# A decoder step on one core: the window's new scores join the other new scores, window rows are requested by GpSimd in front of the pages, and the stored tokens are loaded in two portions

## The chip, the cores and the metric

The kernel runs on one core of a Trainium2 chip. A core has a matrix engine (TensorE, PE in the profile), a vector engine (VectorE, DVE), a scalar engine (ScalarE, ACT), a general engine (GpSimd, POOL) and a queue engine that only issues transfers (SyncE, SP). Each engine works through its own row of instructions in order; semaphores tie them together. Transfers (DMA) can be requested from SyncE, ScalarE or GpSimd. The metric is the device time of one execution in microseconds; less is better.

## What is computed

The reference is one step of a hybrid decoder layer: a prompt of 512 tokens, and 8 other sequences that each get 8 new tokens on top of 2048 stored ones. Two attention branches run side by side, Fox (with forget gates) and NSA (compressed blocks, selected blocks, and a sliding window of 512), then gates merge them, and an MLP follows. What matters here is the part on the 8 sequences:

```python
PAST_LEN = 2048; PAGE_SIZE = 128; DEC_BATCH = 8; DEC_SEQ = 8; WINDOW = 512

def gather_pages(pool, page_table):
    g = pool[page_table]
    return g.reshape((g.shape[0], g.shape[1] * g.shape[2]) + g.shape[3:])

def fox_attend(q, cq, q_pos, k, v, ck, k_pos):
    s = jnp.einsum('btgrd,bsgd->bgrts', q, k).astype(jnp.float32) * HEAD_DIM ** -0.5
    ...
    p = masked_softmax(s + bias, k_pos[None, :] <= q_pos[:, None])
    return jnp.einsum('bgrts,bsgd->btgrd', p.astype(v.dtype), v)

def nsa_attend(q, q_pos, gates, kc, vc, c_end, ks_blk, vs_blk, kw, vw, w_pos):
    ...
    s = jnp.einsum('btgrd,bwgd->bgrtw', q, kw).astype(jnp.float32) * scale - m * dw.astype(jnp.float32)
    p_w = masked_softmax(s, (dw >= 0) & (dw < WINDOW) & (w_pos >= 0)[None, :])
    o_w = jnp.einsum('bgrtw,bwgd->btgrd', p_w.astype(vw.dtype), vw)
    return gates[..., 0:1] * o_c + gates[..., 1:2] * o_s + gates[..., 2:3] * o_w
```

## The kernel before, in words

The stage of the change is `sample_attention`. It handles the 8 sequences one after the other, b = 0 to 7; the sliding window is handled once for each pair, n = b // 2. For one sequence all stored keys and values of two kinds are brought in: Fox rows `fr` and the rows of the selected blocks `sr`, 2.1 MB each. They stand in three row buffers that rotate (b % 3), and are transposed in place by VectorE (`key_turn`) ahead of the scores.

The order on PE for one sequence is: `sequence_scores` (`ss`, 64 matmuls of 32 x 512 on the rows and 4 on `CT`), `new_scores` (`sn`, the new tokens against each other), on even sequences `window_new` (the window's new scores, into the right half of the same bank), then `values` of the sequence before (`so`, with rows and the transposed weights `spT`), on odd sequences the window's values (`so<-wr`) and the sums (`accS`), on even ones `window_keys` (`wk`, transposes of window rows `wr`). Last come the transposes of the softmax weights, `turn_weights` (`spn`, `sp`), which ScalarE copies out of the bank to `TN` and `spT`, and on even sequences the window's scores (`sw`).

`sample_load(b)` requests the rows of a sequence: four 512-KB loads of `fr` and sixteen 128-KB loads of `sr`, half on SyncE's queue and half on GpSimd's, two and eight each. `sample_load(b + 2)` stands behind `values(b - 1)`, whose matmuls are the last to read the buffer. `window_load` requests the window's rows of one sequence (512 KB); for the first pair GpSimd does it ahead of the loop, for the others ScalarE, at the end of an odd iteration. `key_prep` is two GpSimd instructions that prepare the forget counts of one sequence, and stands at the end of an iteration. `key_counts` and `key_turn` are VectorE's work on the next sequence, tied to be issued after the statistics of the current one.

The order of the instructions on an engine is set by a scheduler, which goes by the order of the code, priorities and the `issue_after` ties. A request is tied to the one before it on the same engine (`self.issued`), as `key_prep` is for GpSimd.

At the last sequence the mixer follows. Its input, the stored tokens, stands in DRAM (`hfd`) and is loaded into `hL` in eight parts of 288 KB, alternately by SyncE and GpSimd. ScalarE copies each part to `hH` with reduced digits, VectorE keeps the rest in `hL`. `mix_first` then multiplies the first gate group (`mg00`) in pairs of parts, in between the values of the last sequence; further gate groups (`mg01` and so on) follow in `mix_part`.

## Time and profile before

| what | us |
|---|---|
| median of 3 runs | 1208.71 |
| lowest and highest | 1204.95, 1223.38 |
| the profiled execution | 1212.07 |
| its span, first to last instruction | 1210.4 |
| the eight sequences | about 437 to 569 |

In the stage the windows of the profile, cut about at the scores of the sequences, show these shares of their length:

| window, us | length | PE busy | granted clock | DMA share |
|---|---|---|---|---|
| 437 to 453 | 16 | 14.27 | 0.95 | 1.00 |
| 453 to 470 | 17 | 15.05 | 0.85 | 0.58 |
| 470 to 485 | 15 | 12.13 | 1.00 | 0.99 |
| 485 to 502 | 17 | 15.06 | 1.00 | 0.84 |
| 502 to 515 | 13 | 10.98 | 0.87 | 1.03 |
| 515 to 531 | 16 | 15.07 | 1.00 | 0.98 |
| 531 to 551 | 20 | 15.31 | 0.57 | 0.59 |
| 551 to 569 | 18 | 16.74 | 1.00 | 0.63 |

How to read the views. A timeline row gives the start and duration, the engine, the code's line, the operation, what is written and read, shapes and a count; at its end in brackets stand the idle time of the engine ahead of it and what ended that. "issue" there means that nothing shown in the profile was waited for. PEld is PE's loading of weights. SPq and ACTq are the queues' own instructions, whose transfers land later. A row of waits gives the total in us, the number and the longest. A row of a tile gives count and min/median/max of the duration in ns. The clock is the share of full speed granted to PE. All 16 transfer engines together are a DMA share of 1.00.

### The profile page before, as it was taken

The numbers are of one execution on the slowest core, as the hardware profiler recorded it, in microseconds if no ns is written. First come the engines' busy times: TensorE is split into PE (matmuls) and PEld (weight loads), VectorE is DVE, ScalarE is ACT, GpSimd is POOL, SyncE is SP. The second block draws the span as 40 slices with busy tenths as digits, with TensorE's granted clock in tenths as the row PEclk, the third lists the DMA queues.
The fourth block names the chain that finished last, engine by engine and source line by source line (L and its number), as shares of the span: only waits on it lengthen the run. The fifth ranks groups of instructions, "written<-read, shape, count | busy, mean of one in ns | idle before, by whom it ended". The sixth has DMA issues, their size and how long they took to land. (4 is left out here: it accounts for less than half of the span.)

```text
span 1210.4 us, 24491 instructions
## 1 busy us (share of the span) xinstructions
PE 1134.3 (94%) x9305; PEld 972.1 (80%) x9305; DVE 686.4 (57%) x1743; ACT 508.9 (42%) x1062; POOL 194.5 (16%) x284
## 2 busy tenths in 40 slices
PE   3869999999999988888999999999999999999998
PEld 3867789988666545546999999988988989899896
DVE  6777666675788867656643437652343433333545
ACT  3446553444777644436422324464321313123230
POOL 6530000001211343330000000010201102011110
PEclk9989999999999899989999999999999999999999
DMA  9996485764876597994733333142322314223102
GB/s 222 281 262 179 144 256 187 231 208 129 276 237 202 180 279 264 325 323 133 184 81 94 79 96 106 42 118 85 106 71 70 105 35 137 66 78 97 43 18 79
DMA packets 164488, 184.68 MB, mean 153 GB/s; under 512 B 17386, under 2 KB 143795, under 8 KB 162195
## 3 DMA queue, kind: packets, MB, share of 16 engines
q1 hardware_dynamic: 141954, 137.63, 38.8%
q0 software_dynamic: 10832, 32.12, 8.2%
q10 hardware_dynamic: 11584, 13.37, 3.7%
q8 instruction: 73, 1.20, 0.4%
q14 instruction: 45, 0.36, 0.1%
HBM read 175.17 MB, written 28.81 MB: 169 GB/s over the span
## 5 line engine op out<-in xcount | busy, mean ns | idle before, releaser
L2049 POOL TENSOR_TENSOR u<-u 128x576 f32<-128x576 f32 x32 | 54.0, 1688 | 417.5 <-ACT u L112 327.9
L100 DVE TENSOR_TENSOR acc<-acc,dn 128x512 f32<-128x512 f32 x60 | 39.8, 686 | 78.0 <-PE dn L77 78.0
L77 PE MATMUL mg<-hH,wml 128*128 128x288 f32 x256 | 75.1, 295 | 0.0
L77 PE MATMUL mg<-hH,wmh 128*128 128x288 f32 x256 | 74.9, 295 | 0.0
L77 PE MATMUL mg<-hL,wmh 128*128 128x288 f32 x256 | 72.8, 294 | 0.0
L77 PE MATMUL hid<-xh,w1hlk 128*128 128x256 f32 (+1 forms) x192 | 47.6, 341 | 20.5 <-ACT xh L112 20.5
L783 DVE TENSOR_TENSOR u<-u,u 128x512 fp32r<-128x512 f32 x64 | 28.4, 484 | 63.0 <-ACT u L112 63.0
L77 PE MATMUL z<-winh,h2r 128*128 128x264 f32 (+1 forms) x288 | 57.8, 290 | 2.3 <-ACT adw L112 2.3
L112 ACT ACTIVATE xh<-cpg 128x512 fp32r<-128x512 f32 x64 | 37.4, 623 | 46.1 <-PE hid L77 29.6
L77 PE MATMUL z<-winh,h 128*128 128x264 f32 (+1 forms) x288 | 56.7, 287 | 0.0
L131 DVE TENSOR_TENSOR xl<-cpg,xh 128x512 fp32r<-128x512 f32 x64 | 42.5, 685 | 19.9 <-ACT xh L112 19.6
L131 DVE TENSOR_TENSOR wml<-wmr,wmh 128x1024 fp32r<-128x1024 f32 x16 | 19.6, 1224 | 59.0 <-ACT wmh L112 59.0
L77 PEld LDWEIGHTS hid<-xh,w1hlk 128*128 128x128 f32 x192 | 33.6, 203 | 23.7 <-ACT xh L112 20.5
L77 PE MATMUL hid<-xh,w1hlv 128*128 128x256 f32 (+1 forms) x192 | 47.0, 338 | 5.3 <-ACT csx L112 5.3
L77 PEld LDWEIGHTS z<-winh,h2r 128*128 128x128 f32 x288 | 45.8, 190 | 3.7 <-ACT adw L112 2.5
L77 PEld LDWEIGHTS mg<-hH,wmh 128*128 128x128 f32 x256 | 48.1, 188 | 0.2
L77 PEld LDWEIGHTS mg<-hH,wml 128*128 128x128 f32 x256 | 48.1, 188 | 0.0
L112 ACT ACTIVATE u<-up 128x256 f32<-128x256 f32 (+1 forms) x96 | 27.7, 324 | 46.9 <-PE up L77 46.8
L77 PEld LDWEIGHTS mg<-hL,wmh 128*128 128x128 f32 x256 | 47.3, 188 | 0.0
L77 PEld LDWEIGHTS z<-winh,h 128*128 128x128 f32 x288 | 46.6, 193 | 0.0
L77 PE MATMUL z<-winl,h 128*128 128x264 f32 (+1 forms) x160 | 44.9, 287 | 0.5 <-DVE winl L131 0.5
L459 DVE STREAM_TRANSPOSE cpg<-cpg 128x1024 f32<-128x1024 f32 (+1 forms) x36 | 39.8, 1116 | 9.1 <-DMA cpg<-in_cache_nsa_kv 9.0
(839 smaller groups left out, 3585.8 us busy)
## 6 DMA issues: line engine op xcount, KB each, us to landing
adw<-in_w_ada SPq DMA_DIRECT2D x16, 1024.0 KB
foxD<-in_cache_fox_kv SPq DMA_DIRECT2D x128, 128.0 KB
wur<-in_w_up SPq DMA_DIRECT2D x32, 512.0 KB
wdr<-in_w_down SPq DMA_DIRECT2D x32, 512.0 KB
cpg<-in_cache_nsa_kv SPq DMA_DIRECT2D x64, 128.0 KB
cpg<-in_cache_nsa_kv POOLq DMA_DIRECT2D x64, 128.0 KB, 6.1
wada<-in_w_ada ACTq DMA_DIRECT2D x8, 1024.0 KB
sr<-in_cache_nsa_kv SPq DMA_DIRECT2D x64, 128.0 KB
```

What stands on the lines that cost most here:

```text
L77: ins = self.nc.tensor.matmul(out, a, b, start=start, stop=stop, skip_group_check=True)
L100: self.nc.vector.tensor_tensor(out, a, b, op=op)
L112: return self.nc.scalar.activation(out, in_, f, **kw)
L131: self.splits.append((eng or self.nc.vector).tensor_tensor(l, x, h.bitcast(F32), op=OP.subtract).ins)
L459: self.flipped = self.nc.vector.transpose(v, v).ins
L783: (eng or self.nc.vector).tensor_tensor(h2[:, o:o + n], x[:, i:i + n], h2[:, i:i + n].bitcast(F32), op=OP.subtract)
L2049: nc.gpsimd.tensor_tensor(u[j], u[j], u[j], op=OP.mult)
```

## The change

There are three parts, and two moves that come with them.

1. The window's two new-score matmuls of an even sequence move from `window_new` to `new_scores`, ahead of VectorE's first read of the bank. The operands are the same.
2. `window_load` of the next pair moves from ScalarE's queue, at the end of an odd iteration, to GpSimd's, right behind `window_values`. `sample_load(b + 2)` moves behind it, and `key_prep(b + 2)` moves from the end of the iteration to its start, for sequence 2 ahead of the loop.
3. Of the eight token loads the first two stay where they were. The other six wait for a small ScalarE copy into their target, which is tied behind the last `spT`; the places that it writes are overwritten by the loads.

```diff
@@ new function
+    def tokens_load(self, ks):
+        for k in ks:
+            self.dma("gpsimd" if k % 2 else "sync", self.hL[:, k].bitcast(F32), self.hfd[:, k])
@@ sample_attention, ahead of the loop
         self.key_prep(1)
         self.sample_load(1)
+        self.key_prep(2)
         self.sample_load(2)
@@ in the loop
+            if b and b + 2 < NB:
+                self.key_prep(b + 2)
             self.sequence_scores(b)
             self.new_scores(b)
...
             if b:
                 self.values(b - 1)
-                if b + 2 < NB:
-                    self.sample_load(b + 2)
             if odd:
                 self.window_values(n)
+                if b < last:
+                    for o in range(2):
+                        self.window_load(b + 1 + o, "gpsimd")
                 if b > 1:
                     self.pair_sums(n - 1)
             else:
                 for o in range(2):
                     self.window_keys(b + o)
+            if b and b + 2 < NB:
+                self.sample_load(b + 2)
...
-            if b + 2 < NB:
-                self.key_prep(b + 2)
             if b == last:
...
-                for k in range(NK):
-                    self.dma("gpsimd" if k % 2 else "sync", self.hL[:, k].bitcast(F32), self.hfd[:, k])
+                self.tokens_load(range(2))
...
-            elif b < last:
-                for o in range(2):
-                    self.window_load(b + 1 + o, "scalar")
...
+        with self.tc.issue_after(self.last_weights):
+            self.last_weights = self.act(self.hL[0:1, 2:NK, 0:1], self.T[3][0:1, 0, 0:NK - 2, None]).ins
+        self.tokens_load(range(2, NK))
@@ new_scores
+        if b % 2 == 0:
+            for o in range(2):
+                self.mm(pb[64 * o:64 * o + 64, 64:128], self.queries(b + o)[1], self.knT[:, 2, :], True, True)
...
@@ window_new
-        for o in range(2):
-            self.mm(pn[64 * o:64 * o + 64], self.queries(2 * i + o)[1], self.knT[:, 2, :], True, True)
```

What it moves on the engines, at three places. In each listing a row is one instruction: its line, operation, output, inputs and shape.

First GpSimd at the start of the stage. Here `fr_6387` and `sr_6409` are the rows of sequence 1, `fr_6501` those of sequence 2, and the `wr` are the window rows of sequences 0 and 1:

```order
 L155 DMA wr_6419<-in_state_win_kv 128x1024
 L155 DMA wr_6420<-in_state_win_kv 128x1024
-L1597 COPY D3b<-scr 128x16x16
-L1708 CAST D3b<-Dt 128x16x8
-L1709 TENSOR_TENSOR D3b<-Dt,D3b 128x16x8
+L1601 COPY D3b<-scr 128x16x16
+L1715 CAST D3b<-Dt 128x16x8
+L155 DMA fr_6501<-foxD_81 128x1024
+L1716 TENSOR_TENSOR D3b<-Dt,D3b 128x16x8
 L155 DMA fr_6387<-foxD_80 128x1024
 L162 TENSOR_LOAD ptp
```

GpSimd's first load for sequence 2 now stands ahead of all its loads for sequence 1; before, it came behind the last of them. SyncE's loads keep their order.

Then ScalarE at the sixth sequence, before and after; `sS` and `sN` are the scores in its softmax, `sp` the transposed weights:

```order
L112 ACTIVATE sN_6404,ss_5_7721<-sN_6404,ss_5_7722 128x64
L112 ACTIVATE sS,ss_5_7721<-sS,ss_5_7722 128x1024 x2
L155 DMA wr_6419<-in_state_win_kv 128x1024
L155 DMA wr_6420<-in_state_win_kv 128x1024
L112 ACTIVATE TN<-spn_7952 64x128
L112 ACTIVATE spT_6389<-sp_7955 128x512
```

```order
L112 ACTIVATE sN_6404,ss_5_7723<-sN_6404,ss_5_7724 128x64
L112 ACTIVATE sS,ss_5_7723<-sS,ss_5_7724 128x1024 x2
L112 ACTIVATE TN<-spn_7954 64x128
L112 ACTIVATE spT_6389<-sp_7957 128x512
L112 ACTIVATE spT_6390<-sp_7963 128x512
```

The two requests have left ScalarE. They are on GpSimd now, where at each odd sequence but the last they stand directly ahead of the ten page loads, as here in the iteration of sequence 5:

```order
L155 DMA wr_6419<-in_state_win_kv 128x1024
L155 DMA wr_6420<-in_state_win_kv 128x1024
L155 DMA fr_6387<-foxD_86 128x1024
L162 TENSOR_LOAD ptp
L155 ISA
L155 DMA sr_6409<-in_cache_nsa_kv 128x256
```

Before, `fr_6387` stood behind a page load of the previous sequence there, with nothing between. Last, PE at the end of the stage, before and after; `mg_8492` and `mg_8493` before, and `mg_8493` and `mg_8494` after, are the first gate group (`mg00`), `mg_8605` and `mg_8606` the next one (`mg01`):

```order
L77 MATMUL mg_8493<-hH,wml_0_8378 128x288
L77 MATMUL mg_8492<-hH,wmh_0_8377 128x288
L77 MATMUL mg_8492<-hH,wml_0_8378 128x288
L77 MATMUL mg_8493<-hH,wmh_0_8377 128x288
L77 MATMUL mg_8493<-hH,wml_0_8378 128x288
```

```order
L77 MATMUL mg_8494<-hH,wml_0_8372 128x288
L77 MATMUL mg_8605<-hH,wmh_0_8558 128x288
L77 MATMUL mg_8606<-hH,wmh_0_8558 128x288
L77 MATMUL mg_8493<-hH,wmh_0_8371 128x288
L77 MATMUL mg_8493<-hH,wml_0_8372 128x288
L77 MATMUL mg_8494<-hH,wmh_0_8371 128x288
```

After the eight matmuls on the first two tokens' parts, 23 of the next gate group are now mixed in between the rest of the first.

## The prediction, as recorded before the result

> **What bounds the kernel now.** I read the page first, then PE's waits in the stage of the change, then PE's own rows in order of time, and last the two-microsecond windows.

> ```profile
> span 1210.4 us, 24491 instructions
> PEclk9989999999999899989999999999999999999999
> ```

> The profiled execution took 1212.07 us, 1.67 us more than its span; the median of the runs shown is 1208.71. The clock row is nearly whole, so what can be won is idle PE time or a stretch at half clock. The waits of PE between 435 and 600 us:

> ```profile
> PE so L77 <- issue: 5.8, 4, 3.0
> PE sn L77 <- DVE ss L1749: 5.0, 4, 1.3
> PE ss L77 <- ACT spT L112: 4.1, 2, 3.3
> PE ss L77 <- DMA sr<-in_cache_nsa_kv: 0.6, 1, 0.6
> ```

> The second row is the wait that part one of the change removes: four times 1.3 us. Whether it is worth 5.0 us depends on what sets the next step. PE's timeline (start, duration):

> ```profile
> 459.78 1.06 PE L77 MATMUL ss<-fr,scr 32*32 32x512 f32 x8
> 461.78 0.63 PE L77 MATMUL ss<-sr,scr 32*32 32x512 f32 x4 [0.93 <-DVE sr L1719]
> 469.23 0.32 PE L77 MATMUL so<-vnew,TN 64*32 64x64 f32 x8
> 473.42 1.06 PE L77 MATMUL ss<-fr,scr 32*32 32x512 f32 x8 [0.82 <-ACT spT L112]
> 480.38 0.34 PE L77 MATMUL sn<-knT,bdN 128*64 128x64 f32 x4 [1.28 <-DVE ss L1749]
> 488.51 0.63 PE L77 MATMUL ss<-fr,scr 32*32 32x512 f32 x4 [0.58 <-DMA sr<-in_cache_nsa_kv]
> 498.26 0.32 PE L77 MATMUL so<-vnew,TN 64*32 64x64 f32 x8
> 518.08 0.63 PE L77 MATMUL ss<-fr,scr 32*32 32x512 f32 x4
> 526.20 0.32 PE L77 MATMUL so<-vnew,TN 64*32 64x64 f32 x8
> 534.83 1.91 PE L77 MATMUL ss<-fr,scr 32*32 32x512 f32 x5 [3.32 <-ACT spT L112]
> 554.84 0.63 PE L77 MATMUL ss<-fr,scr 32*32 32x512 f32 x4
> 571.89 0.25 PE L77 MATMUL so<-sr,spT 128*32 128x64 f32 x2 [3.00 <-issue]
> 572.82 0.40 PE L77 MATMUL mg<-hH,wmh 128*128 128x288 f32 x1
> ```

> The scores `ss` of sequences 1, 2, 3, 5, 6 and 7 begin at 459.78, 473.42, 488.51, 518.08, 534.83 and 554.84. The `so<-vnew` rows end the reading of a row buffer, after which its next rows are requested: sequence 0's ends at 469.55, and the scores of 3, which use that buffer, begin 18.96 us later; sequence 2's ends at 498.58, and the scores of 5 begin 19.50 us later. VectorE says why, just ahead of both:

> ```profile
> 487.70 0.71 DVE L1719 STREAM_TRANSPOSE fr<-fr 128x512 f32<-128x512 f32 x1 [1.39 <-DMA fr<-foxD]
> 517.26 0.71 DVE L1719 STREAM_TRANSPOSE fr<-fr 128x512 f32<-128x512 f32 x1 [0.32 <-DMA fr<-foxD]
> ```

> So odd scores start when rows have landed, and PE idle time ahead of them is cover. The third odd step is different: 36.8 us from the scores of 5 to those of 7, against 26.7 and 29.6. ScalarE and the windows (us, PE, PEld, DVE, ACT, POOL, clock, DMA share, GB/s) show the cause:

> ```profile
> 527.80 0.19 ACT L112 ACTIVATION_READ_ACCUMULATOR sS<-sS,ss 128x1 f32 x1
> 533.16 0.82 ACTq L155 DMA_DIRECT2D wr<-in_state_win_kv  x2
> 534.02 0.27 ACT L112 ACTIVATE TN<-spn 64x128 f32<-64x128 f32 x1 [6.03 <-DMA sr<-in_cache_nsa_kv]
> ```
> ```profile
> 490.00:492.00 2.00, 2.00 (x35) 0.59 (x30) 0.99 (x6) 0.87 (x2) 1.54 (x3) 1.00 1.04 389
> 508.00:510.00 2.00, 0.81 (x24) 0.69 (x28) 1.93 (x9) 0.45 (x3) 0.54 (x1) 0.83 1.01 374
> 538.00:540.00 2.00, 2.00 (x17) 0.28 (x2) 0.00 (x0) 0.00 (x0) 0.00 (x0) 0.50 1.06 389
> 568.00:570.00 2.00, 0.89 (x63) 0.73 (x52) 1.13 (x2) 2.00 (x5) 0.00 (x0) 1.00 0.97 352
> ```

> ScalarE stands from 527.99 to 533.16 on the request for window rows, which waits for an earlier page load; the copies `spT` stand behind it, PE waits 3.32 us for them, and the clock is then 0.50. In the window at 538 PE is full but runs 17 matmuls where the one at 490 has 35: at this rate 68 score matmuls take 8.0 us in place of 3.9.

> **The change part by part.**

> *New scores together.* On even sequences two matmuls move ahead of VectorE's read. They cost nothing more (four rows in 0.34 us, still issued) and PE's 1.28-us wait goes, four times. The work behind it is values and window keys, and behind these the odd scores, which waited for rows at 488.51. A buffer comes free earlier by the gap only if the step ahead wasn't set by rows; for the odd chain it was. I take 0 for the first three; the fourth (sequence 6) lies in the step costed next, where the rows again come last. Ends: 0 and -5.0.

> *Window rows to GpSimd.* The six requests leave ScalarE. In the third step nothing then stands between 527.99 and `spT`; PE starts the scores of 6 about 3.3 us earlier and at full clock. What is late next is the rows of 7: sequence 4's buffer is free at 526.52, plus the mean of 18.96 and 19.50, 19.2, gives 545.7. PE's own path agrees: 534.83-3.32 = 531.5, plus the 15.1 us from the scores of 2 to those of 3, gives 546.6, or 545.3 without the 1.28-us gap. Against 554.84 that is -9.1. Ends: -3.3 (the wait alone, if the clock falls anyway) and -10.4 (with the last gap too).

> The requests now stand on GpSimd in front of ten page requests of the same iteration. Each takes about what the rows there show:

> ```profile
> L155 POOL DMA_DIRECT2D sr<-in_cache_nsa_kv x64: 536/536/548, 415.5 to 534.1; - x64
> DMA to landing us min/median/max: 5.2/6.7/8.6
> ```

> Two of them are 1.08 us in front of GpSimd's half of the pages, which SyncE's half need not wait for. The bytes (1.05 MB) had to come in either case; only their place among the pages changes, at 365 GB/s (the windows show 363 to 389) 2.9 us of the whole bus. As the pair of sequences is needed only two iterations on, each load bought in front costs the next odd scores between -1 (no request left to compete with later pages) and 2.9 us (all bytes in front). I take 0.5 three times, half of the issue time, since the copies of SyncE's half cover the rest: +1.5, ends -3 and +9.

> [...]

> *Rows of sequence 2 in front of those of 1.* The order of GpSimd's requests also changes at the stage's start, though the diff's lines for sequences 1 and 2 only add a key preparation: the first Fox load of sequence 2 (`fr2`) now precedes the ten loads of sequence 1. SyncE and GpSimd there:

> ```profile
> 438.90 0.43 SPq L155 DMA_DIRECT2D fr<-foxD  x1
> 447.67 1.91 SPq L155 DMA_DIRECT2D sr<-in_cache_nsa_kv  x4
> ```
> ```profile
> 439.59 0.57 POOL L155 DMA_DIRECT2D fr<-foxD  x1
> 449.43 1.14 POOL L155 DMA_DIRECT2D sr<-in_cache_nsa_kv  x2 [3.91 <-issue]
> 450.62 0.54 POOL L155 DMA_DIRECT2D fr<-foxD  x1
> ```
> ```profile
> SPq L155 <- PE ofox L77: 7.8, 1, 7.8
> ```

> SyncE's first load into the same fresh buffers waited 7.8 us for the prompt attention's last matmul, till 447.67. GpSimd's load of `fr2` waits for PE too; now the ten loads of sequence 1 (issued 439.59 to 450.57) stand behind it. Ten requests of 0.54 us from 447.7 end at 453 without another stall, at 459 with the 11.0 us they took before; with 6.7 us to land, the last rows are in at 460 to 466. The scores of 1 began at 459.78; by 35 matmuls in 2 us and the 0.93-us gap their last quarter began at about 463.6. I take +2 (the middle, 463, then a transpose of 0.7 us and the remaining matmuls); ends 0, and +9 if the rows come at 466 and the PE wait costs the scores their clock as at 534.83 (another 4.1). The shift is passed on whole, since sequence 0's values stand behind these scores.

> *Tokens in two portions.* Two of eight token loads stay; six (1.77 MB) are issued after ScalarE's last `spT`.

> ```profile
> L155 POOL DMA_DIRECT2D hL<-hfd x4: 536/536/545, 562.7 to 564.3; - x4
> DMA to landing us min/median/max: 3.4/7.0/8.6
> 571.64 1.26 ACT L112 ACTIVATE hH<-hL 128x576 fp32r<-128x576 f32 x2 [1.08 <-DMA hL<-hfd]
> ```
> ```profile
> 577.98 2.28 PE L77 MATMUL mg<-hL,wmh 128*128 128x288 f32 x16
> ```

> PE's 3.00-us stall at 568.9 lies where the bus is full of tokens (0.97 in the window at 568); I count it as gone. Against it, the second portion lands 3.4 to 7.0 us after about 568.6, is split in 0.6 us, and can be used from 572.6 to 576.2. Until then PE has the rest of the values, eight matmuls on the first tokens and 23 pulled forward of the next gate group, 0.1325 us each from the row above, 4.1 in all: up to about 573.4. Before, PE idled 3.0 us and about 1.4 more up to 576; now 0 to 2.8, so -4.4 to -1.6. Six loads go out at once, which speaks for the late landing: I take -2.3; ends -4.4 and +1 (the stall returning with the later transfers).

> Sum: 0 - 9.1 + 1.5 + 2 - 2.3 = -7.9, so 1212.07 - 7.9 = 1204.2, or 1204; 0.4% below the median shown.

> **The rivals.**

> A, *the wait at the start costs the clock.* Held to 447.7, GpSimd's half of sequence 1 lands at 466, PE idles some 4 us and the scores run at 0.50: +9 in place of +2, so 1204 + 7 = 1211. For it: 533 to 550, where a 3.32-us wait did so. Against: SyncE's half lands on time, so the scores can begin in pieces. [...]

> B, *everything named as idle really goes.* Gaps (-5.0, of which 1.3 is in the third step), third step -10.4, tail -4.4, no cost at the start or on GpSimd: -3.7 - 10.4 - 4.4 = -18.5, so 1194. For it: even scores wait for no rows. Against: the two rows of VectorE at 487.70 and 517.26.

> C, on the other side: *window rows in front of the pages.* If GpSimd's share of the bus is half, 1.05 MB in front of its pages holds them 5.7 us, at each of the three loads: 17.2 in place of 1.5, and 1204 + 15.7 = 1220. It makes the kernel slower than before from 3.1 us per load on (9.4 in place of 1.5 takes up the 7.9). For it: odd scores wait for rows, and GpSimd carries half of them. Against: SyncE's half then has the bus to itself, and both halves must land.

> D, *nothing comes of it:* the third step's wait reappears as a wait for rows, the time stays at 1212 less the tail, 1210. It lies within A's span.

> **How the numbers follow.** The forecast (1198 to 1208) 0.49; A with D (1208 to 1216) 0.25; B (1188 to 1198, the lower end with 3 us won by the window loads and a margin as large) 0.15; C (1216 to 1225) 0.08; anything else 0.03. The range 1193 to 1217 leaves out half of B, most of C and the rest: 0.17. Two per cent, about what a measurement of this kernel can tell from no change, is 24 us: below 1185 lies a part of the rest and B's far end, 0.02; above 1233 a part of C and of the rest, 0.03; within, 0.95.

> **What the changed profile would show.** Right: no wait of `sn` for VectorE; no request of window rows on ScalarE's queue and `spT` right behind the softmax at the sixth sequence; 27 to 29 us between the scores of 5 and 7, at full clock; SyncE's 7.8-us wait for `ofox` now seen on GpSimd too, and the scores of 1 waiting 1 to 3 us for rows; the values of 7 without a stall and the gate matmuls of two groups mixed. Wrong: another stretch at 0.50, odd scores more than 20.5 us behind the values that freed their buffer (C), or steps shorter than 18.9 us (B).

## The result

The changed kernel is slower: 1223.84 us median over 20 runs (1215.2 to 1236.77) against 1212.85 over 20 runs of the kernel before (1204.95 to 1227.12). The ratio is 1.0088, with a 95% interval of 1.0059 to 1.0116. Ratios compare the fast runs alone, those within 1.5% of their kernel's fastest, and the medians are of all runs, so the two need not agree to the last digit. The predicted 1204 was below the kernel before, and its range ended at 1217.

The profiled execution took 1225.08 us, close to its median. Its page's first line and clock row:

```profile
span 1223.4 us, 24489 instructions
PEclk9979999999999997788999999999999999999999
```

Slices 16 to 19, which hold the sequences from 1 on, show 7, 7, 8, 8 where the kernel before had one 8 and nines. PE's waits in the same stretch as before, 435 to 600 us:

```profile
PE ss L77 <- DVE fr L1726: 5.8, 2, 3.9
PE ss L77 <- DVE map L100: 5.5, 1, 5.5
PE so L77 <- issue: 3.4, 4, 1.7
PE mg L77 <- ACT hH L112: 2.1, 1, 2.1
...
PE ss L77 <- DMA wbr<-in_w_br_fox: 1.6, 1, 1.6
PE ss L77 <- DVE sd L1812: 1.3, 1, 1.3
```

The waits of `sn` (5.0 us) and for `spT` (4.1 us) are gone as announced, but PE now waits 14.2 us ahead of scores (four of these rows), where it waited 5.6 us before, with the 4.1 for `spT` among them. PE's timeline shows that these stand ahead of every odd sequence's scores:

```profile
457.99 1.93 PE L77 MATMUL ss<-fr,scr 32*32 32x512 f32 x8 [5.51 <-DVE map L100]
...
472.95 0.32 PE L77 MATMUL so<-vnew,TN 64*32 64x64 f32 x8
...
494.30 1.06 PE L77 MATMUL ss<-fr,scr 32*32 32x512 f32 x8 [3.87 <-DVE fr L1726]
...
508.55 0.44 PE L77 MATMUL so<-vnew,TN 64*32 64x64 f32 x8
...
528.42 1.06 PE L77 MATMUL ss<-fr,scr 32*32 32x512 f32 x8 [1.97 <-DVE fr L1726]
...
541.34 0.32 PE L77 MATMUL so<-vnew,TN 64*32 64x64 f32 x8
...
560.51 1.28 PE L77 MATMUL ss<-fr,scr 32*32 32x512 f32 x8 [1.64 <-DMA wbr<-in_w_br_fox]
```

From the first of these matmuls to the last, the scores of 1, 3, 5 and 7 take 10.9, 9.1, 8.9 and 10.4 us, where the kernel before took 6.6, 5.3, 5.3 and 4.7. In the windows the clock is at 0.50 through most of each, from the first matmul at sequence 1 and from 1.3, 1.4 and 3.4 us behind it at 3, 5 and 7, though PE is full in them:

```profile
442.00:444.00 2.00, 2.00 (x28) 0.95 (x32) 0.98 (x2) 0.64 (x2) 0.54 (x2) 1.00 0.02 6
466.00:468.00 2.00, 2.00 (x24) 0.22 (x8) 0.00 (x0) 0.00 (x0) 0.00 (x0) 0.50 0.03 8
498.00:500.00 2.00, 2.00 (x22) 0.66 (x26) 0.90 (x3) 0.00 (x0) 0.00 (x0) 0.50 1.06 365
532.00:534.00 2.00, 2.00 (x22) 0.70 (x26) 0.94 (x3) 0.00 (x0) 1.07 (x2) 0.50 1.06 385
566.00:568.00 2.00, 2.00 (x18) 0.56 (x26) 1.31 (x4) 0.00 (x0) 0.00 (x0) 0.50 0.00 0
```

The first row shows the start: at 442 the transfers stand still (share 0.02). GpSimd and SyncE at that place:

```profile
443.44 0.53 POOL L155 DMA_DIRECT2D fr<-foxD  x1 [9.15 <-PE ss L77]
444.39 0.57 POOL L155 DMA_DIRECT2D fr<-foxD  x1
```
```profile
442.94 1.91 SPq L155 DMA_DIRECT2D sr<-in_cache_nsa_kv  x4
```

GpSimd waits 9.15 us with its load for sequence 2, and sequence 1's loads begin behind it at 444.39.

Stage for stage, counted from the end of the prompt attention's last matmul (447.62 before, 442.89 after; what lies ahead differs between executions of one kernel), the two profiled executions stand so:

| | before, us | after, us | difference |
|---|---|---|---|
| scores of 1 begin | 12.2 | 15.1 | +2.9 |
| values of 0 end | 21.9 | 30.4 | +8.5 |
| scores of 3 begin | 40.9 | 51.4 | +10.5 |
| values of 2 end | 51.0 | 66.1 | +15.1 |
| scores of 5 begin | 70.5 | 85.5 | +15.0 |
| values of 4 end | 78.9 | 98.8 | +19.9 |
| scores of 7 begin | 107.2 | 117.6 | +10.4 |
| first gate matmul | 125.2 | 139.3 | +14.1 |
| last gate matmul begins | 275.2 | 293.6 | +18.4 |

Between the start of the scores of 1, 3 and 5 and the end of the values behind them the loss grows by 5.6, 4.6 and 4.9 us. That is mostly the half clock: the scores alone are longer by 4.3, 3.8 and 3.6 us. From the scores of 7 to the first gate matmul it grows by 3.7. Besides, 2.9 us come at the start, 2.0 ahead of the scores of 3 and 4.3 in the gate groups. The one gain, 9.5 us, is the step of sequence 6, where ScalarE no longer stands on its request.

### The profile page after: what moved, and what is told of

It is laid out like the page before. It is cut to its first block, busy times and chain, and to the rows that moved or that the text cites. A ratio compares the mean times of both kernels' runs of the same rounds, so it can differ in the third digit from the quotient of the medians.

```text
span 1223.4 us, 24489 instructions
## 1 busy us (share of the span) xinstructions
PE 1147.9 (94%) x9305; PEld 975.0 (80%) x9305; DVE 687.5 (56%) x1743; ACT 508.9 (42%) x1063; POOL 197.5 (16%) x290
## 4 chain that ended last, share of the span: by engine, by line
PE 77%; DMA 6%; issue 5%; DVE 5%; ACT 4%; POOLq 1%; POOL 1%; SPq 1%; ACTq 0%; DVEq 0%
PE dn L77 17%; PE up L77 16%; PE z L77 9%; PE mg L77 8%; PE wo L77 4%; PE br L77 4%; PE hid L77 3%; PE ss L77 3%; DMA sr<-in_cache_nsa_kv 2%; DMA cpg<-in_cache_nsa_kv 2%; PE ada L77 2%; DMA fr<-foxD 1%; PE so L77 1%; DMA x<-in_x_prompt 1%; PE owin L77 1%
## 5 line engine op out<-in xcount | busy, mean ns | idle before, releaser
L77 PE MATMUL mg<-hH,wmh 128*128 128x288 f32 x256 | 75.7, 298 | 2.3 <-ACT hH L112 2.1
L77 PE MATMUL mg<-hH,wml 128*128 128x288 f32 x256 | 75.8, 298 | 0.0
L77 PE MATMUL mg<-hL,wmh 128*128 128x288 f32 x256 | 73.1, 296 | 0.0
L77 PE MATMUL hid<-xh,w1hlk 128*128 128x256 f32 (+1 forms) x192 | 47.3, 339 | 20.1 <-ACT xh L112 20.1
L112 ACT ACTIVATE xh<-cpg 128x512 fp32r<-128x512 f32 x64 | 37.4, 623 | 50.0 <-PE hid L77 31.9
L77 PE MATMUL z<-winh,h2r 128*128 128x264 f32 (+1 forms) x288 | 57.4, 288 | 0.0
L77 PE MATMUL z<-winh,h 128*128 128x264 f32 (+1 forms) x288 | 55.7, 283 | 0.0
L77 PE MATMUL ss<-fr,scr 32*32 32x512 f32 x256 | 41.0, 754 | 13.0 <-DVE fr L1726 5.8
L77 PE MATMUL hid<-xh,w1hlv 128*128 128x256 f32 (+1 forms) x192 | 48.3, 345 | 4.9 <-ACT csx L112 4.9
L77 PEld LDWEIGHTS hid<-xh,w1hlk 128*128 128x128 f32 x192 | 33.5, 203 | 23.3 <-ACT xh L112 20.1
L77 PEld LDWEIGHTS mg<-hH,wmh 128*128 128x128 f32 x256 | 48.7, 191 | 2.9 <-ACT hH L112 2.4
L77 PEld LDWEIGHTS mg<-hH,wml 128*128 128x128 f32 x256 | 48.7, 191 | 0.0
L77 PEld LDWEIGHTS mg<-hL,wmh 128*128 128x128 f32 x256 | 47.6, 190 | 0.0
L112 ACT ACTIVATE u<-up 128x256 f32<-128x256 f32 (+1 forms) x96 | 27.7, 324 | 47.3 <-PE up L77 47.3
L77 PEld LDWEIGHTS z<-winh,h2r 128*128 128x128 f32 x288 | 45.5, 189 | 1.2 <-issue 0.4
L77 PEld LDWEIGHTS z<-winh,h 128*128 128x128 f32 x288 | 45.7, 189 | 0.0
L77 PE MATMUL z<-winl,h 128*128 128x264 f32 (+1 forms) x160 | 44.4, 284 | 0.5 <-DVE winl L131 0.5
```

What stands on the lines that cost most here:

```text
L77: ins = self.nc.tensor.matmul(out, a, b, start=start, stop=stop, skip_group_check=True)
L112: return self.nc.scalar.activation(out, in_, f, **kw)
```

## The experiments

The theories have letters of their own; W is the prediction's rival C. S: the start's order (rows of 2 in front of those of 1) costs the first 8 us. C: PE's waits for rows, no longer broken up by the `sn` waits, lower the clock, and the odd scores then run at half speed. W: window loads in front of the pages make the rows late. Ratios are to the kernel before on the same chip, with 95% intervals; the experiments e1 to e14 ran on four chips.

**Rows in order.** The broken order comes from a tie: each GpSimd load is issued behind the last tied GpSimd instruction, and `key_prep(2)`, which is ready early, had taken that place from the loads of sequence 1. Edit to the changed kernel:

```diff
+        end = self.issued["gpsimd"]
         self.key_prep(2)
+        self.issued["gpsimd"] = end
         self.sample_load(2)
```

> The changed kernel, but GpSimd's first load for sequence 2 stands behind all its loads for sequence 1 again, as before the change. Theory S (the start): the transfer engines no longer idle at the last prompt matmuls, the scores of 1 begin about 12 us after the last ofox matmul in place of 15.1 and at full clock, and the time falls by 6 to 9 us. Theory W (window loads in front of pages cost most): the time falls by less than 3 us, and the waits ahead of the odd scores stay as they are.

Ratio 0.9990 (0.9959 to 1.0020), 1209.81 us: against the changed kernel's 1.0088 the order at the start is worth 0.98%, some 12 us, more than the 6 to 9 expected. The scores of 1 begin 10.9 us after the last `ofox` matmul, and the transfer share at 442 to 444 is 1.01. Half of the expectation was wrong: these scores still run at half clock, after a wait of only 1.3 us in their midst, and so do those of 3 and 5:

```profile
PE ss L77 <- DMA sr<-in_cache_nsa_kv: 3.0, 1, 3.0
PE ss L77 <- DVE fr L1728: 2.3, 1, 2.3
...
PE ss L77 <- DVE map L100: 1.3, 1, 1.3
```

**Filled waits.** Edit to the changed kernel, with further matmuls of the window's score form, whose output nobody reads:

```diff
                 self.window_scores(n)
+                self.warm(b, (8, 6, 4, 4)[n])
...
+    def warm(self, b, n):
+        pb = self.trb(f"warm{b}")
+        for o in range(n):
+            with self.tc.issue_after(self.last_mm):
+                self.mm(pb[64 * (o % 2):64 * (o % 2) + 64, :], self.queries(b + o % 2)[1], self.wkt[o % 2], True, True)
```

> The changed kernel with 8, 6, 4 and 4 further matmuls of the window's score form behind the window's scores of the four pairs, into a bank that nobody reads; they fill part of PE's wait for rows ahead of the odd scores and compute nothing that is used. Theory C (the clock): the granted clock stays near 1.0 through the odd scores and the time falls by 8 to 16 us, though PE has 6 us more work. Theory R (rows and transfers alone set the pace): the clock rises, but the next odd scores wait as much longer, and the time stays within 3 us or grows.

Ratio 1.0026 (0.9995 to 1.0056), 1215.86 us, 0.62% below the changed kernel (7.5 us, just short of the 8 to 16 of theory C) though the start's order is still wrong and PE has more to do. In the profiled execution, the fastest of its 12 runs, all odd scores run at full clock (4.7 to 6.4 us each). The fill isn't free: the median of the runs' clocks is the highest of the first four experiments, 0.9775, but the time is above that of the run before it.

**New scores apart.** The two window matmuls go back into `window_new`, behind VectorE's read; the rest of the change stays.

```diff
-        if b % 2 == 0:
-            for o in range(2):
-                self.mm(pb[64 * o:64 * o + 64, 64:128], self.queries(b + o)[1], self.knT[:, 2, :], True, True)
...
         pn = self.snb[:, 64:128]
+        for o in range(2):
+            self.mm(pn[64 * o:64 * o + 64], self.queries(2 * i + o)[1], self.knT[:, 2, :], True, True)
```

> The changed kernel without its first part: the window's new scores again follow VectorE's read of the bank, with PE's 1.28-us waits back. If those waits broke up PE's idle time and kept the clock, the odd scores run at full clock and the time falls by 4 us or more. If they were covered by the wait for rows, as the prediction has it, the time stays within 2 us and the waits ahead of odd scores shrink by 1.28 us. If they were worth their length, the time grows by about 5 us.

Ratio 1.0010 (0.9983 to 1.0037), 1215.87 us: with the four 1.28-us waits back the kernel is 0.78% faster, some 9 us. Two odd scores are at half clock in place of four. Those of 3 wait 3.92 us (3.87 in the changed kernel, so the 1.28 us did not come off this wait), those of 5 no longer wait:

```profile
494.51 1.45 PE L77 MATMUL ss<-fr,scr 32*32 32x512 f32 x8 [3.92 <-DVE fr L1726]
...
528.99 0.63 PE L77 MATMUL ss<-fr,scr 32*32 32x512 f32 x4
```

**Window loads on ScalarE.** They go back to the end of the odd iterations:

```diff
-                if b < last:
-                    for o in range(2):
-                        self.window_load(b + 1 + o, "gpsimd")
...
+            elif b < last:
+                for o in range(2):
+                    self.window_load(b + 1 + o, "scalar")
```

> The changed kernel, with the window's loads back on ScalarE's queue at the end of the odd iterations. Theory W: rows land about 2 us sooner behind the values that free their buffer (19 in place of 21 us at sequence 3), and the time falls by 3 us or more. Against it the prediction's step: ScalarE's stall on the request comes back at sequence 5, and the time grows by 5 to 9 us.

Ratio 1.0137 (1.0090 to 1.0185), 1227.56 us over six runs: 0.49% above the changed kernel, with intervals that overlap. W has no support here. The scores of 3 begin 21.4 us behind the values that free their buffer with the loads on ScalarE, and 21.0 with them on GpSimd, so the later rows (18.96 us before the change) aren't the window loads' doing; whether the move of `sample_load` makes them later wasn't tested. 37.2 us pass from the scores of 5 to those of 7, as many as the 36.8 before the change.

The next runs take the parts apart. **New scores alone** is the kernel before with the first part only, the edit being the third one above reversed.

> The kernel before with the first part of the change alone. If taking the 1.28-us waits away bundles PE's idle time ahead of odd scores also where rows arrive as they did before, more of the odd scores run at half clock and the time grows by 3 to 9 us. If that needs the late rows of the changed kernel, the time stays within 3 us. If the waits were worth their length, it falls by 3 to 5 us.

Ratio 0.9974 (0.9940 to 1.0008), 1214.56 us: nothing that can be told from no change (the median before is 1213.29 on this chip), and its runs spread from 1202.36 to 1227.27. The profiled one (1218.57) has four scores at half clock, after waits of 1.3 to 3.91 us; over all its runs the median granted clock is 0.9725, about the 0.973 of the kernel before.

**Without new scores, in order** joins the edits of the first and third experiments.

> The changed kernel without its first part and with GpSimd's loads of sequences 1 and 2 in the old order: window loads on GpSimd and tokens in two portions remain. If the start and the bundled waits are separate losses, both are won: 8 us below either of the runs that undo one alone, that is about 1203. If both act through the same half clock, undoing the second wins little more: 1207 to 1211.

Ratio 0.9937 (0.9908 to 0.9966), 1204.41 us. That is near the 1203 of two separate losses: against the run in order alone it wins 0.53%, with intervals that just overlap. No odd score runs at half clock.

**Window loads on GpSimd alone** also puts all eight token loads back to their old place:

```diff
-                self.tokens_load(range(2))
+                self.tokens_load(range(NK))
...
-        with self.tc.issue_after(self.last_weights):
-            self.last_weights = self.act(self.hL[0:1, 2:NK, 0:1], self.T[3][0:1, 0, 0:NK - 2, None]).ins
-        self.tokens_load(range(2, NK))
```

> The run before this one also without the token portions, so only the window loads on GpSimd remain of the change. The prediction's step for sequence 5 gives 9 us less than the kernel before, 1203, if rows land as soon as they did. By the prediction's term for the tokens this is 2 us more than with the portions; if the portions' wait for the second part costs more than it saves, it is 1 to 4 us less.

Ratio 0.9918 (0.9886 to 0.9950), 1202.67 us. This is the second part of the change by itself, with the moves that come with it and the old order at the start, and it beats both kernels. PE's waits and the scores of 5 and 7:

```profile
PE sn L77 <- DVE ss L1755: 5.0, 4, 1.3
...
PE ss L77 <- DVE sr L1725: 0.9, 1, 0.9
PE ss L77 <- ACT spT L112: 0.8, 1, 0.8
```
```profile
514.63 1.06 PE L77 MATMUL ss<-fr,scr 32*32 32x512 f32 x8
...
542.27 0.63 PE L77 MATMUL ss<-fr,scr 32*32 32x512 f32 x4
```

27.6 us pass between these, and the scores of 5, 6 and 7 run at full clock. The second half of sequence 2's scores does not, though PE waited only 0.81 us ahead of them:

```profile
467.81 1.06 PE L77 MATMUL ss<-fr,scr 32*32 32x512 f32 x8 [0.81 <-ACT spT L112]
...
471.14 1.08 PE L77 MATMUL ss<-fr,scr 32*32 32x512 f32 x4
```

A row of the second half takes 1.08 us there, where one of the first takes 0.63.

**In order, filled** is the first experiment with `warm` for the first three pairs, 2, 4 and 4 matmuls.

> The changed kernel with GpSimd's loads in the old order and 2, 4 and 4 unused matmuls behind the window's scores of the first three pairs, 1.1 to 2.2 us each where PE waited 1.3, 3.0 and 2.3 us in the run that only restored the order. If the half clock of these three odd scores is what is left, the time falls by 6 to 10 us against that run, to about 1202. If the fill costs as much as the clock gives, it stays at 1208 to 1212.

Ratio 0.9919 (0.9888 to 0.9950), 1206.53 us, 0.71% below the run that only restored the order, with all parts of the change in it and all odd scores at full clock.

**Tokens alone** is the kernel before with the third part only.

> The kernel before with the third part alone: two token loads early, six behind the last weights. The prediction's term is a gain of 2.3 us between the last weight transposes and the end of the gate groups; against it, the runs so far show that stretch as long with the portions as without (154.5 to 158.2 against 155.3 to 156.0 us). If the latter holds, the time stays within 2 us.

Ratio 1.0030 (1.0005 to 1.0056), 1214.05 us: the portions cost about 3.6 us (0.6 to 6.8 by the interval), where the expectation had at most 2 either way. PE waits for the second portion where it did not wait before:

```profile
PE ss L77 <- ACT spT L112: 4.7, 2, 3.8
PE mg L77 <- ACT hH L112: 2.2, 1, 2.2
```

The first row is ScalarE's stall on its window request, still there in this kernel. In the profiled executions the stretch from the last weight transposes to the last gate matmul is hardly longer with portions (154.6 to 158.2 us in eight) than without (154.5 to 156.4 in seven), so where the rest of the 3.6 us lies wasn't found.

**New scores and window loads, in order**, without the token portions:

> The changed kernel without the token portions and with GpSimd's loads in the old order: new scores together and window loads on GpSimd. If the bundled waits are what the first part costs, odd scores at half clock come back as in the run that only restored the order and the time is 4 to 8 us above the window loads alone, which took 1202.7. If the first part costs nothing here, it stays within 2 us of them.

Ratio 1.0001 (0.9963 to 1.0038), 1213.79 us. **The window loads alone once more**, beside it:

> The window loads on GpSimd alone once more, beside the two runs above on the same chip: 1202 to 1204, with all odd scores at full clock.

Ratio 0.9900 (0.9865 to 0.9936), 1201.58 us, no score of sequences 1 to 7 at half clock. So with the window loads on GpSimd the first part costs 0.8 to 1.0%, about 10 to 12 us. The median granted clock of the runs, 0.9725 against 0.981, accounts for most of it: a share of 0.0085 of 1208 us is 10 us, an estimate for a PE that is always busy. The two profiled executions took the same (1207.96 and 1208.09 us; the latter is the slowest of its six and runs sequence 0's first scores at half clock), but from the scores of 1 to the end of those of 7 they need 101.9 and 92.0 us. The profile of the former shows two scores at half clock, behind waits such as

```profile
PE ss L77 <- DVE fr L1725: 3.7, 2, 2.1
```

The first part also moves a VectorE read: the window's new scores are read ahead of the sequence's statistics, where they were read behind them. Two runs tell this from the waits. **The old order on VectorE**, from the kernel of e10:

```diff
-            if not odd:
-                self.window_new(n)
             self.sequence_max(b)
+            if not odd:
+                with self.tc.issue_after(self.last_stat):
+                    self.window_new(n)
```

> New scores together and window loads on GpSimd, in order, as in e10, but VectorE reads the window's new scores behind the statistics of the sequence, where it read them before the change. If the first part costs by VectorE's earlier read, the time returns to that of the window loads alone, 1202. If it costs by PE's bundled waits, it stays at e10's ratio of 1.000, within 0.004.

Ratio 1.0049 (1.0018 to 1.0080), 1216.35 us: the read isn't the cost. **The same kernel as e10, filled** with 2, 4, 4 and 4 matmuls by `warm`:

> The kernel of e10 with 2, 4, 4 and 4 unused matmuls behind the window's scores of the four pairs. If the first part costs by bundled waits that lower the clock, all odd scores run at full clock and the ratio falls from e10's 1.000 by 0.004 to 0.009. If VectorE's earlier read is the cost, it stays at 1.000 or above.

Ratio 0.9913 (0.9881 to 0.9945), 1204.16 us, all odd scores at full clock, and the median granted clock of the runs is 0.9845. Useless matmuls in the place of the waits bring back the whole loss of the first part.

**Dense matmuls within the scores.** The last question was why the clock stays low through ten microseconds in which PE is never idle. Edit to the changed kernel, in `sequence_scores` behind the first half:

```diff
+            if h == 0 and b % 2:
+                pb = self.trb(f"dense{b}")
+                for o in range(8):
+                    with self.tc.issue_after(self.last_mm):
+                        self.mm(pb[64 * (o % 2):64 * (o % 2) + 64, :], self.queries(b)[1], self.wkt[o % 2], True, True)
```

> The changed kernel with 8 unused matmuls on 128 rows in the middle of each odd sequence's scores, which otherwise are matmuls on 32 rows and 32 columns. If it is those small matmuls that leave the clock at half once a wait has lowered it, the second half of the scores runs at full clock, 2.5 us in place of 5. If the low clock lasts a fixed time whatever PE does, the second half stays at 4 to 5 us.

In sequence 1 the first half of the scores begins at 460.51 and runs at 0.50; the dense matmuls follow from 467.19 to 473.31, and the second half takes 2.4 us, at full clock. PE's timeline and two windows:

```profile
467.19 6.12 PE L77 MATMUL dense<-wkt,bdN 128*64 128x512 f32 x16
475.12 0.49 PE L77 MATMUL ss<-CT,W 32*128 32x512 f32 x2
```
```profile
470.00:472.00 2.00, 2.00 (x8) 0.51 (x6) 0.00 (x0) 0.00 (x0) 0.00 (x0) 0.50 0.00 0
474.00:476.00 2.00, 2.00 (x32) 0.73 (x17) 0.36 (x1) 0.00 (x0) 0.00 (x0) 1.00 0.03 8
```

The clock comes back some 5 us after the dense matmuls begin (3.4 and 5.2 us at sequences 3 and 5, whose second halves also take 2.4 us). The single run took 1238.49 us; the dense work is on PE's path.

Together, the scores of sequences 1 to 7 whose second half ran at half clock in the profiled execution of each kernel, how many of them are odd ones, the median granted clock of all its runs, and its ratio:

| kernel | half-clock scores | odd | clock of the runs | ratio |
|---|---|---|---|---|
| before | 1 | 0 | 0.973 to 0.975 | 1 |
| the change | 4 | 4 | 0.967 | 1.0088 |
| in order (e1) | 3 | 3 | 0.9755 | 0.9990 |
| filled (e2) | 0 | 0 | 0.9775 | 1.0026 |
| without part one (e3) | 2 | 2 | 0.970 | 1.0010 |
| without part two (e4) | 4 | 3 | 0.9635 | 1.0137 |
| part one alone (e5) | 4 | 3 | 0.9725 | 0.9974 |
| parts two and three, in order (e6) | 1 | 0 | 0.9775 | 0.9937 |
| part two, in order (e7, e11) | 1, 0 | 0, 0 | 0.9785, 0.981 | 0.9918, 0.9900 |
| in order, filled (e8) | 0 | 0 | 0.982 | 0.9919 |
| part three alone (e9) | 2 | 0 | 0.972 | 1.0030 |
| parts one and two, in order (e10) | 2 | 2 | 0.9725 | 1.0001 |
| the same, old VectorE order (e13) | 2 | 2 | 0.971 | 1.0049 |
| the same, filled (e14) | 0 | 0 | 0.9845 | 0.9913 |

One profiled execution doesn't stand for all runs of a kernel (e2 and e5 show it), but no kernel with a ratio below 0.995 has an odd score at half clock, and their runs have the highest clocks of the table, 0.9775 and more, which only e2 reaches besides.

## Why the prediction was wrong

**New scores together, taken as 0, bounded by 0 and -5.0.** This step failed, and its sign was outside the bounds. The reading behind it held on the whole: PE's idle time ahead of odd scores is cover, and the removed 1.28-us waits came back as waits for rows (e10's odd scores wait 6.5 us in all, those of e7 and e11 0.9 and 3.9, for 5.0 us of `sn` waits removed). What the step overlooked is that an idle time has a price that depends on what runs behind it. Behind an `sn` wait stand dense values: the clock fell around 9 of the 18 `sn` waits of sequences 2, 4 and 6 in the six profiles of the table that have them, but was back after 3.4 us (seven times) or 6.8 (twice). A fall ahead of scores or within them lasted 10.2 to 17.1 us in each of the 26 cases of the table. With window loads on GpSimd the part costs about 1% (e10 against e11), and filling the wait returns all of it (e14). Alone, on the kernel before, no cost could be told, nor a lower clock over all runs (e5); why it doesn't show there isn't settled.

**Rows of sequence 2 in front, taken as +2, bounded by 0 and +9.** The place and the mechanism were right, the size wasn't: +8.5 us to the end of sequence 0's values in the profile, and in the runs 0.98%, some 12 us, above even the upper bound (e1). Rival A said what it would take, idle time that costs the clock, and gave it 0.25 together with D. The argument against it, that SyncE's half would let the scores begin in pieces, failed: PE stood still for 5.51 us.

**Window rows to GpSimd, -9.1 and +1.5.** Right as to the mechanism. From the scores of 5 to those of 7 it forecast 27.6 us (545.7 less 518.08); with the part alone it is 27.6 by e7's profile. That they agree so closely is luck: e11, the same kernel, takes 26.9, and in e7 the scores of 7 don't wait for rows, which by the forecast come last. In the changed kernel, with the scores of 5 and 7 at half clock, it is 32.1. The whole part is worth -0.8 to -1.0%, 10 to 12 us against a forecast of 7.6. In the changed kernel the softmax's end and the copy behind it show the stall gone (ScalarE's timeline):

```profile
541.99 0.19 ACT L112 ACTIVATION_READ_ACCUMULATOR sS<-sS,ss 128x1 f32 x1
543.62 0.28 ACT L112 ACTIVATE TN<-spn 64x128 f32<-64x128 f32 x1 [1.44 <-PE spn L83]
```

The +1.5 for pages held back, and with it rival C, found no support: its sign, odd scores more than 20.5 us behind the values, showed once (21.0 at sequence 3), but e4 has the loads on ScalarE, and there its rows come no sooner (21.4). GpSimd's requests of window rows are about as short as its page requests, which take 536 to 548 ns in the changed kernel:

```profile
L155 POOL DMA_DIRECT2D wr<-in_state_win_kv x8: 533/542/557, 432.6 to 543.1; - x8
```

The eight requests took 533 to 557 ns, and the move was the part that paid.

**Tokens, -2.3.** Wrong in sign where the part stands alone: +0.3% (0.05 to 0.56%). The 3.00-us stall did go, but PE then waits for the second portion, 2.15 us in the changed kernel. In the company of other parts no effect can be told (e6 against e7, e1 against e10).

Some readings in the prediction are off, but none of them carries the error. From the scores of 1 to those of 3 its rows give 28.7 us, not 26.7; the row of 16 gate matmuls in 2.28 us gives 0.1425 us each, not 0.1325; and the windows that it shows move 352 to 389 GB/s.

The chain of kernels from the one before over e7 and e11, e10 and e1 to the change splits the 0.88% into part two -0.9%, part one +0.9%, part three -0.1% and the start's order +1.0%. As differences of neighbours they add up by construction. Part one alone (-0.3%), part two (-0.9%), part three alone (+0.3%) and the start's order (+1.0%) come to +0.1%, short of the 0.88% measured, so what a part is worth seems to depend on the others.

## What to carry to other kernels

An idle time that hides behind a later wait isn't worth nothing: before it is removed, look at what runs right behind the wait that grows. If that work can't bring the clock up again, as the scores here didn't in 49 of 49 steps that they filled at half clock, a wait ahead of it can cost more than waits of the same sum elsewhere (0.8 to 1.0%, e10 against e7 and e11), and a few useless matmuls in it can be the cheaper form (14 of them in e14, ratio 0.9913 against e10's 1.0001). When a step that is ready early is put into a chain of ties, check each queue's order: here one line of key preparation let a load overtake ten others, which cost 0.98% (e1).

## What the runs showed of the hardware

Among the scores of sequences 1 to 7 in the 16 profiled executions, 28 stood behind a wait of 1.3 to 5.5 us or held one, and 26 of these ran at half clock, many only from some way in; the exceptions waited 1.64 (e10) and 2.44 us (e13). The length of the wait is no threshold, though: in e6, e7 and e9 the second half of sequence 2's scores ran at half clock behind 0.81 us.

The score matmuls on 32 rows and 32 columns did not bring the clock back: of the steps that they filled (3.2 us or more), all 49 at half clock were followed by another at half clock, and all 47 at full clock by another at full clock. In the changed kernel they ran at half clock for 7.1 to 10.9 us of full PE. Behind such scores the clock came back 2.7 to 6.0 us after their end, where matmuls on 128 rows follow, and in e12 3.4 to 5.2 us after the dense ones began.
